# Three 256-column matmuls into one set of PSUM columns in place of a 512- and a 256-column matmul into two halves

## The chip, the cores and the metric

The kernel runs on one core of a Trainium2 chip. The metric is the device time of one execution in microseconds. Before the change it is 2729.07 us, the median of three runs (2727.39 to 2730.07).

## The reference

The reference is a forward pass of two different transformer-like blocks in float32 over 256 tokens of 2048 features, one after the other.

```python
# first block
h = rms_norm(x, norm_mix_g); proj = h @ w_in                 # 2048 x 14336
y_a = attention(q, k, v, rel_table) @ w_attn_o
y_b = rg_lru_branch(xr, gr, ...) @ w_lru_o
y_c = short_conv_branch(sc_b, sc_c, sc_x, ...) @ w_sc_o
x = x + (g_a * y_a + g_b * y_b + g_c * y_c) @ w_out          # gates: sigmoid(g_pre + gate_b)
x = x + square(relu(rms_norm(x, norm_mlp_g) @ w_mlp_up)) @ w_mlp_down
x = rms_norm(x, final_g)
# second block
h = rmsnorm(x, g_mix) @ w_in                                 # SSD, gate z, indexer, q, k, v
x = x + concat(y_ssd, y_att) @ w_out
x = x + square(relu(rmsnorm(x, g_mlp) @ w_up)) @ w_down      # 2048 x 8192 x 2048
```

Nearly all of the arithmetic is in the products of 256 tokens with weight matrices of 2048 rows or more.

## The kernel before

Activations are kept feature-major: a k-tile is 128 features by 256 tokens (T = 256). The products want more precision than one pass of TensorE gives in float32r, so both sides are split into a high and a low part. `Operand` holds the activations as [hi | lo], 512 columns per k-tile, and `stream` loads the weights (`raw`), makes `hi` on ScalarE (a cast) and `lo` on VectorE (a subtraction). Three products are added up: hi hi, hi lo and lo hi.

The work is a list of jobs. A job is a group of 512 output columns; its k-tiles come in chunks of two, 256 rows by 512 columns of the weight matrix, 512 KB in one transfer. `stream` walks over all chunks of all jobs; at each step it issues loads some steps ahead, splits the weights of a chunk ahead, calls `products` for the first pair of accumulators (`ps[0]`, 2 x 128 output features) and then for the second (`ps[1]`), and in between lets a stage of side work through (`side.tick`: norms, attention, recurrences) and a stage of the evacuations under way (`advance`). The evacuations are generators: each `yield` hands over until the next call of `advance`. The order of all instructions is the order in which they are emitted; a rough model of the engines' clocks (`Meter`) decides when side work is emitted.

A weight tile is 128 x 128 weights of one k-tile. Its weights are the stationary operand and the activations move past them. For each tile `products` issues two matmuls: `hi` of the weights against both halves of the activations, 512 columns, and `lo` of the weights against the high half, 256 columns, into the second half of the accumulator. An accumulator for 128 features is thus 512 columns of PSUM, a whole bank: the first half has hi hi, the second hi lo and lo hi. A pair of them takes two banks, and the pool `psm` has three such pairs; two more banks (`pss`) serve the side work.

When a group ends, `total` adds the halves: ScalarE copies the second half to `cr`, VectorE adds the first half to it and writes `tot`. What follows reads `tot`: a multiplication by the reciprocal norm (`keep`, `gate`), by a gate (`gated`), an addition to the residual (`residual`), a squared relu (`relu2`).

Jobs marked `tok` are token-major: the activations are stationary, the weights move, and all three products have 512 columns. These are the values of both attentions and the last quarter of the last product. In the trace all instructions of the engines have the line of one helper (L104), so that groups are told apart by their tiles: `ps<-h,hi` is a 512-column matmul of weights `hi` with operand `h`, and `ps<-h,lo` the 256-column one. `hm` is the operand of the products up, `hid` that of the products down; `mixop`, `ymix`, `ya`, `yb` and `yc` are those of the other products.

Of the kernel before, what the change touches and what calls it, by code (L numbers as in the profile page):

```python
# [10 lines left out]
F32 = mybir.dt.float32  # L11
# [14 lines left out]
# how far the vector and scalar engines may fall behind for side work, and shortly before a group of columns ends  # L26
MOST, LEAST = 9.0, 7.0
# what a stage of side work yields if the next one waits for nothing that the vector and scalar engines owe
FREE = "free"
# lanes of side work, the urgent ones first  # L30
LANES = ["norm", "small", "idx", "gate", "ssd", "k", "q", "att"]
# the second block's projections: SSD input, its gate z, indexer queries, queries, keys, values
# [3 lines left out]
class Operand:  # L36
    """Feature-major activations split exactly into two float32r parts: [hi | lo] per k-tile."""
# [20 lines left out]
class Job:  # L58
    """One group of output columns: chunks of two k-tiles stream past pairs of accumulators."""
# [9 lines left out]
class Meter:  # L69
    """An engine whose instructions are timed, roughly, as they are emitted: each starts when the engine is free and  # L70
    what it reads has been written."""
# [36 lines left out]
class Core:  # L108
# [8 lines left out]
    def behind(self):  # L117
        """How far the vector or scalar engine is behind the tensor engine."""
        return max(self.vector.clock, self.scalar.clock) - self.tensor.clock


class Side:
    """Work that runs between the steps of the main stream, in lanes: a lane's next stage is emitted once what its
    last one computes is ready, and while the vector and scalar engines aren't behind."""
# [20 lines left out]
    def bank(self, name):  # L145
        """The side banks take turns: the one that is next, free once its last tile has been read."""
        self.banks.append(name)
        old = self.banks.popleft()
        if old:
            self.core.free[name] = self.core.read.get(old, 0.0) + Meter.LATENCY  # L150
# [24 lines left out]
class Builder:  # L175
    def __init__(self, ctx, tc, d):
# [7 lines left out]
        self.psm = pool("psm", 3, space=PSUM)  # L184
# [21 lines left out]
    def vectors(self, name, st, specs):  # L206
        """Per-feature vectors, laid out as [feature in its tile, tile], by one transpose of their rows."""
# [12 lines left out]

    def wload(self, w, col):
        """Chunks of two k-tiles by 512 columns of w, from column col."""
        def load(raw, c):
            src = w[2 * P * c:2 * P * (c + 1), col:col + 512].rearrange("(k p) n -> p k n", p=P)
            self.nc.sync.dma_start(raw, src)
        return load

    def stream(self, jobs):
# [5 lines left out]
        for s, (j, c, i) in enumerate(steps):  # L234
# [26 lines left out]
            if first:  # L261
                ps = [self.psm.tile([P, 2, 512], F32, tag="main", name=f"ps{s}_{q}") for q in range(npair)]
                held = []
            op = j.op() if callable(j.op) else j.op
            # around a group's ends its first pair runs a step ahead, so that it starts and ends earlier
# [19 lines left out]
    def products(self, j, op, ps, q, c, hi, lo, first, last):  # L285
        """Two k-tiles past a pair of accumulators: hi hi, hi lo and lo hi."""
        nc = self.nc
        for m in range(2):
            o = ps[:, m, :]
            for kk in range(2):  # L290
# [9 lines left out]
                if a:  # L300
                    nc.tensor.matmul(o, hi[:, kk, w], op.both(k), start=True, stop=False)
                nc.tensor.matmul(o[:, T:], lo[:, kk, w], op.hi(k), start=False, stop=False)
                if not a:
                    nc.tensor.matmul(o, hi[:, kk, w], op.both(k), start=False, stop=z)

    def advance(self, newest=False, only=None):
        """One stage of the evacuations under way, or of the newest."""
# [10 lines left out]

    def total(self, ps, t=None):
        """The sum of both halves of a pair of accumulators."""  # L320
        nc = self.nc
        cr = self.tmp.tile([P, 2, T], F32, tag="cr", name="cr")
        nc.scalar.copy(cr, ps[:, :, T:])
        if t is None:
            t = self.tmp.tile([P, 2, T], F32, tag="tot", name="tot")
        nc.vector.tensor_tensor(t, ps[:, :, :T], cr, op=OP.add)
        return t
# [4 lines left out]
    def split(self, op, k, src):  # L332
        """k-tiles k and k + 1 of op from src [P, 2, T]."""
# [4 lines left out]
    def split_scaled(self, op, k, src, g):  # L338
        """k-tiles k and k + 1 of op from src times the per-feature g."""
# [13 lines left out]
    def squares(self, acc, k, src, g=None):  # L353
        """Adds the squares of a pair of tiles to acc [P, 2, T]."""
# [13 lines left out]
    def mean(self, acc, out=None, scale=1.0 / D):  # L368
        """Sums of the columns of acc times scale, token-major [P, 2]."""
# [9 lines left out]
    def rsqrt(self, out, v):  # L379
        """out = (v + EPS) ** -0.5, small: a guess from the exponent's bits, then Newton."""  # L380
# [13 lines left out]
    def row(self, out, col):  # L394
        """out [P, T] = col [P tokens, 2] laid along the free axis of every partition."""
# [16 lines left out]

    def load_x(self, load):
        """x, turned feature-major: h = x * norm_mix_g as an operand, x itself kept in DRAM."""
# [60 lines left out]
    def keep(self, dst, at, func=None, scaled=True):  # L475
        """Evacuates to tiles at + 2q of dst, times rstd, through func."""
        def evac(q, ps):
            k = at + 2 * q
            o = dst[k // 4][:, k % 4:k % 4 + 2, :]
            if not scaled:  # L480
                self.total(ps, o)
                return
            t = self.total(ps)
            yield
            self.side.drain("norm")
            self.nc.vector.tensor_tensor(t if func else o, t, self.pairwise(self.rstd), op=OP.mult)
# [4 lines left out]
    def keep_tok(self, dst, at):  # L491
        """Evacuates token-major to columns at of dst[token tile]."""
        def evac(q, ps):
            for t in range(2):
                self.nc.scalar.activation(dst[t][:, at:at + 512], ps[:, t, :], AF.Copy, scale=self.rstd_t[:, t:t + 1])
            yield
        return evac

    def gate(self, col, gt):
        """sigmoid(proj + gate_b)"""  # L500
        def evac(q, ps):
            nc = self.nc
            t = self.total(ps)
            g = gt()[:, 2 * q:2 * q + 2, :]
            yield
            nc.vector.tensor_tensor(t, t, self.pairwise(self.rstd), op=OP.mult)
# [5 lines left out]
    def gated(self, gt, mix, j, first, out=None):  # L512
        """mix += gate * y; with out, the sum is split into that operand."""
        def evac(q, ps):
            nc = self.nc
            t = self.total(ps)
            m = mix[j][:, 2 * q:2 * q + 2, :]
            g = gt()[:, 2 * q:2 * q + 2, :]
            yield
            if first:  # L520
                nc.vector.tensor_tensor(m, t, g, op=OP.mult)
            else:
                nc.vector.tensor_tensor(t, t, g, op=OP.mult)
# [6 lines left out]
    def t5_bias(self):  # L530
        """rel_table by distance, masked above the diagonal: [q, head, (128 keys of tile 0 | 256 of tile 1)]."""
# [12 lines left out]
        # 128 copies, 385 apart: read 384 apart, each query's row is the one before it moved by one key  # L544
# [12 lines left out]
    def softmax_rows(self, s):  # L557
        """Rows of s [P, 384]: queries of tile 0 over 128 keys, of tile 1 over 256; in place."""
# [16 lines left out]
    def probs(self, q, k, scale, bias, pt):  # L575
        """Transposed softmax of one head, into pt [P, 384]: scale(token tile), bias(token tile) [P, keys]."""
# [14 lines left out]
    def weigh(self, pt, v, out, k):  # L591
        """out tile k = v^T p^T, feature-major; v(token tile) is [tokens, 128 features]."""
# [19 lines left out]
    def causal_conv(self, out, src, w, bias, taps, col):  # L612
        """out [P, n, T] = causal depthwise convolution of src [P, n, T], two feature tiles at a time; w(tap) and bias
        per feature tile."""
# [18 lines left out]
    def lru_constants(self):  # L633
        """c4 = 4 softplus(-lambda): log a = -2 c4 r."""
# [14 lines left out]
    def log1p(self, out, e, z, z2):  # L649
        """log(1 + e) for 0 <= e <= 1, as 2 atanh(e / (2 + e))."""  # L650
# [21 lines left out]
    def lru(self, hf, xr, hs):  # L672
# [14 lines left out]
        # a = exp(-2 c4 r), and sqrt(1 - a^2) = (1 + a) sqrt(tanh(c4 r))  # L687
# [44 lines left out]
    def residual(self, j, scale=None, gvec=None, sq=(), op=None):  # L732
        """res += product (times scale); then squares and the next operand, res times gvec."""
        def evac(q, ps):
            nc = self.nc
            t = self.total(ps)
            yield
            k = 4 * j + 2 * q
            r = self.res[j][:, 2 * q:2 * q + 2, :]
            if scale is not None:  # L740
                nc.vector.tensor_tensor(t, t, self.pairwise(scale()), op=OP.mult)
            nc.vector.tensor_tensor(r, r, t, op=OP.add)
# [7 lines left out]
    def relu2(self, hidden, j):  # L750
        def evac(q, ps):
            nc = self.nc
            t = self.total(ps)
            nc.vector.scalar_tensor_tensor(t, t, 0.0, t, op0=OP.max, op1=OP.mult)
# [103 lines left out]
    def output(self, w, op, gvec, wait=None):  # L858
        """res += w^T op, then the operand of the feed-forward; with wait, each half of op for all columns in turn."""
# [38 lines left out]
    def feed_forward(self, up, down, last=None, after=None):  # L898
        """res += relu(hm up)^2 down times the squared reciprocal norm; last(j) prepares the next operand, or without
        it the last quarter is stored."""  # L900
# [25 lines left out]
    def first_end(self):  # L926
        """Evacuation of the first block: the last norm's and the next norm's statistics, the next operand."""
# [487 lines left out]
```

## Time and profile before

| what | value |
|---|---|
| time, median of 3 runs | 2729.07 us (2727.39 to 2730.07) |
| span of the profiled execution | 2727.0 us |
| TensorE (PE) busy | 2704.5 us, 99%, 15382 matmuls |
| weight loads (PEld) busy | 2345.9 us, 86%, 15382 loads |
| VectorE (DVE) busy | 1728.0 us, 63% |
| ScalarE (ACT) busy | 1281.9 us, 47% |
| mean granted TensorE clock | 0.999 |
| mean DMA traffic | 188 GB/s |

The span is the time from the first to the last instruction of one profiled execution, and the device time of a run has a little around it. Busy times are the union of an engine's instructions. Matmuls overlap in the pipeline, so the mean duration of one is longer than the distance from one start to the next; what a matmul costs is read from distances between starts, or from how many fit into a stretch without gaps. A group of instructions is followed by the idle time of its engine just before it and by what ended that idle time.

### The profile page before, as it was taken

Reading aid. Unit: us, or ns where it says so; the run is one execution under the profiler, and the core shown is the slowest. Engines: PE = TensorE matmul, PEld = TensorE weight load, DVE = VectorE, ACT = ScalarE, POOL = GpSimd, SP = SyncE. Lnnn points to the kernel's source line nnn. Section 1 sums busy time; section 2 is a strip of 40 time slices with the busy share of each in tenths; the row PEclk is TensorE's granted clock in tenths of the full one; section 3 lists DMA queues with packets and bytes.
Section 4 is the critical chain, followed back from the end, with each engine's and each line's share of the span. In section 5 each row is a group of like instructions: output and inputs, shape, how many; then the busy total and the mean of one; then the engine's idle time right before and its main releaser. Section 6 shows DMA issues by size and latency. Waiting matters only on the chain.

```text
span 2727.0 us, 38618 instructions
## 1 busy us (share of the span) xinstructions
PE 2704.5 (99%) x15382; PEld 2345.9 (86%) x15382; DVE 1728.0 (63%) x2331; ACT 1281.9 (47%) x1705; POOL 35.0 (1%) x70
## 2 busy tenths in 40 slices
PE   8999999999999999999999999999999999999999
PEld 7788888888888888888888888788888888888887
DVE  7565655656676655555566679687785555555554
ACT  5654544434555443444444455455564344344442
POOL 2000000000000000000000000000000000000000
PEclk9999999999999999999999999999999999999999
DMA  8755555655675656556565557455565555655644
GB/s 283 199 172 173 183 193 190 200 181 184 194 236 180 185 183 210 170 185 201 181 205 174 196 156 235 134 183 187 177 185 183 196 185 179 203 177 190 189 149 168
DMA packets 268660, 513.71 MB, mean 188 GB/s; under 512 B 22994, under 2 KB 23250, under 8 KB 268480
## 3 DMA queue, kind: packets, MB, share of 16 engines
q1 hardware_dynamic: 263360, 496.30, 56.8%
q0 software_dynamic: 4512, 12.84, 1.8%
q8 instruction: 121, 1.98, 0.3%
q10 hardware_dynamic: 608, 2.11, 0.2%
q14 instruction: 59, 0.48, 0.1%
HBM read 503.29 MB, written 7.88 MB: 187 GB/s over the span
## 4 chain that ended last, share of the span: by engine, by line
PE 96%; DMA 3%; issue 1%; DVE 1%; SPq 0%; ACT 0%; POOL 0%; DVEq 0%; POOLq 0%
PE ps L104 93%; DMA t5d<-by 1%; DMA raw<-w_in 1%; PE ix L104 0%; PE sc L104 0%; PE pv L104 0%; DMA bias<-t5d 0%; PE ps_row L104 0%; PE py L104 0%; PE pT L104 0%; PE hn L104 0%; DVE lo L104 0%; PE xT L104 0%; PE lg L104 0%; PE ps_mean L104 0%
## 5 line engine op out<-in xcount | busy, mean ns | idle before, releaser
L104 DVE TENSOR_TENSOR lo<-raw,hi 128x1024 fp32r<-128x1024 f32 (+1 forms) x944 | 1101.9, 1216 | 153.8 <-ACT hi L104 152.4
L104 ACT CAST hi<-raw 128x1024 fp32r<-128x1024 f32 (+1 forms) x944 | 926.6, 1044 | 80.4 <-DMA raw<-w_down 43.1
L104 PE MATMUL ps<-h,hi 128*128 128x512 f32 x2336 | 814.5, 396 | 7.4 <-DVE tot L104 5.6
L104 PE MATMUL ps<-hm,hi 128*128 128x512 f32 x2048 | 705.4, 394 | 0.0
L104 ACT COPY cr<-ps 128x512 f32<-128x512 f32 x241 | 141.3, 587 | 1093.9 <-PE ps L104 1093.9
L104 PE MATMUL ps<-h,lo 128*128 128x256 f32 x2336 | 635.3, 282 | 4.1 <-DVE lo L104 4.1
L104 DVE TENSOR_TENSOR tot<-ps,cr 128x512 f32<-128x512 f32 x230 | 158.4, 691 | 731.5 <-ACT cr L104 731.3
L104 PE MATMUL ps<-hid,hi 128*128 128x512 f32 x1792 | 615.0, 394 | 0.0
L104 PE MATMUL ps<-hm,lo 128*128 128x256 f32 x2048 | 548.5, 278 | 0.0
L104 PEld LDWEIGHTS ps<-h,hi 128*128 128x128 f32 x2336 | 430.9, 188 | 97.7 <-DVE tot L104 6.5
L104 PE MATMUL ps<-hid,lo 128*128 128x256 f32 x1792 | 478.3, 277 | 0.0
L104 PEld LDWEIGHTS ps<-h,lo 128*128 128x128 f32 x2336 | 441.2, 189 | 23.1 <-DVE lo L104 5.0
L104 PEld LDWEIGHTS ps<-hm,hi 128*128 128x128 f32 x2048 | 375.9, 188 | 78.2
L104 PEld LDWEIGHTS ps<-hm,lo 128*128 128x128 f32 x2048 | 384.8, 188 | 11.4
L104 PEld LDWEIGHTS ps<-hid,hi 128*128 128x128 f32 x1792 | 328.6, 188 | 68.3
L104 PEld LDWEIGHTS ps<-hid,lo 128*128 128x128 f32 x1792 | 336.4, 188 | 9.9
L104 PE MATMUL ps<-ymix,hi 128*128 128x512 f32 x256 | 89.3, 397 | 0.0
L104 PE MATMUL ps<-mixop,hi 128*128 128x512 f32 x256 | 87.9, 394 | 0.0
L104 PE MATMUL ps<-hi,hid 128*128 128x512 f32 x256 | 79.0, 389 | 0.0
L104 PE MATMUL ps<-mixop,lo 128*128 128x256 f32 x256 | 68.3, 277 | 0.0
L104 PE MATMUL ps<-ymix,lo 128*128 128x256 f32 x256 | 67.3, 283 | 0.0
L104 PE MATMUL ps<-hi,h 128*128 128x512 f32 x192 | 61.5, 395 | 0.0
(304 smaller groups left out, 1776.3 us busy)
## 6 DMA issues: line engine op xcount, KB each, us to landing
raw<-w_in SPq DMA_DIRECT2D x312, 512.0 KB, 4.1
raw<-w_mlp_up SPq DMA_DIRECT2D x128, 512.0 KB, 4.0
raw<-w_mlp_down SPq DMA_DIRECT2D x128, 512.0 KB, 4.6
raw<-w_up SPq DMA_DIRECT2D x128, 512.0 KB, 4.3
raw<-w_down SPq DMA_DIRECT2D x128, 512.0 KB, 4.5
raw<-w_out SPq DMA_DIRECT2D x64, 512.0 KB, 4.5
raw<-w_attn_o SPq DMA_DIRECT2D x16, 512.0 KB, 4.7
raw<-w_lru_o SPq DMA_DIRECT2D x16, 512.0 KB, 4.1
```

What stands on the lines that cost most here:

```text
L104: return f(out, *args, **kw)
```

## The change

In a tile of a job that is not token-major, `products` issues three matmuls of 256 columns, all into the same 256 columns of PSUM: `hi` of the weights with the high half, `lo` with the high half, `hi` with the low half. The two accumulators of a pair share a bank, so only the first matmul of the first of them has the start flag. `psm` has six tiles of one bank. `total` is gone: what followed it reads PSUM itself, mostly as the first operand of the VectorE instruction. In `relu2` ScalarE writes the relu of the sum to SBUF and VectorE multiplies the sum in PSUM by it, one step later. Token-major jobs get two tiles of one bank each; their matmuls stay as they are. The diff without its changes of comments, cut:

```diff
-        self.psm = pool("psm", 3, space=PSUM)
+        self.psm = pool("psm", 6, space=PSUM)
...
-                ps = [self.psm.tile([P, 2, 512], F32, tag="main", name=f"ps{s}_{q}") for q in range(npair)]
+                ps = [self.main_ps(f"ps{s}_{q}", j.tok) for q in range(npair)]
...
-            o = ps[:, m, :]
+            o = ps[m] if j.tok else ps[:, m, :]
...
-                if a:
-                    nc.tensor.matmul(o, hi[:, kk, w], op.both(k), start=True, stop=False)
-                nc.tensor.matmul(o[:, T:], lo[:, kk, w], op.hi(k), start=False, stop=False)
-                if not a:
-                    nc.tensor.matmul(o, hi[:, kk, w], op.both(k), start=False, stop=z)
+                nc.tensor.matmul(o, hi[:, kk, w], op.hi(k), start=a and m == 0, stop=False, skip_group_check=True)
+                nc.tensor.matmul(o, lo[:, kk, w], op.hi(k), start=False, stop=False, skip_group_check=True)
+                nc.tensor.matmul(o, hi[:, kk, w], op.lo(k), start=False, stop=z and m == 1, skip_group_check=True)
...
-    def total(self, ps, t=None):
-        nc = self.nc
-        cr = self.tmp.tile([P, 2, T], F32, tag="cr", name="cr")
-        nc.scalar.copy(cr, ps[:, :, T:])
-        if t is None:
-            t = self.tmp.tile([P, 2, T], F32, tag="tot", name="tot")
-        nc.vector.tensor_tensor(t, ps[:, :, :T], cr, op=OP.add)
-        return t
+    def main_ps(self, name, tok):
+        if tok:
+            return [self.psm.tile([P, 512], F32, tag="main", name=f"{name}_{t}") for t in range(2)]
+        return self.psm.tile([P, 2, T], F32, tag="main", name=name)
+    def tot(self):
+        return self.tmp.tile([P, 2, T], F32, tag="tot", name="tot")
...
             if not scaled:
-                self.total(ps, o)
+                self.nc.scalar.copy(o, ps)
                 return
-            t = self.total(ps)
-            yield
             self.side.drain("norm")
-            self.nc.vector.tensor_tensor(t if func else o, t, self.pairwise(self.rstd), op=OP.mult)
+            t = self.tot() if func else o
+            self.nc.vector.tensor_tensor(t, ps, self.pairwise(self.rstd), op=OP.mult)
+            yield
             if func:
                 self.nc.scalar.activation(o, t, func)
...
-            t = self.total(ps)
-            yield
             k = 4 * j + 2 * q
             r = self.res[j][:, 2 * q:2 * q + 2, :]
+            t = ps
             if scale is not None:
-                nc.vector.tensor_tensor(t, t, self.pairwise(scale()), op=OP.mult)
-            nc.vector.tensor_tensor(r, r, t, op=OP.add)
+                t = self.tot()
+                nc.vector.tensor_tensor(t, ps, self.pairwise(scale()), op=OP.mult)
+                yield
+            nc.vector.tensor_tensor(r, t, r, op=OP.add)
+            if scale is None:
+                yield
...
-            t = self.total(ps)
-            nc.vector.scalar_tensor_tensor(t, t, 0.0, t, op0=OP.max, op1=OP.mult)
+            t = self.tot()
+            nc.scalar.activation(t, ps, AF.Relu)
+            yield
+            nc.vector.tensor_tensor(t, ps, t, op=OP.mult)
             yield
             self.split(hidden, 4 * j + 2 * q, t)
```

`gate` and `gated` change in the same way as `keep`: the multiplication reads `ps`, and the `yield` comes after it.

## Rows read from the trace of the kernel before

**Rows 1.** The page, busy us (share of the span) x instructions of each engine.

```profile
PE 2704.5 (99%) x15382; PEld 2345.9 (86%) x15382; DVE 1728.0 (63%) x2331; ACT 1281.9 (47%) x1705; POOL 35.0 (1%) x70
```

**Rows 2.** Waits of PE: who waited for whom, us in total, times, longest.

```profile
PE ps L104 <- DVE tot L104: 5.6, 2, 5.1
```

**Rows 3.** View by windows: stretch, length, busy us (x instructions) by engine, PEclk, DMA.

```profile
600.00:900.00 300.00, 300.00 (x1732) 262.24 (x1731) 195.77 (x230) 147.89 (x199) 2.15 (x4) 1.00 0.61 197
```

**Rows 4.** Timeline of PE, operand hm: start us, duration us, instruction, count.

```profile
1499.71 0.39 PE L104 MATMUL ps<-hm,hi 128*128 128x512 f32 x1
1499.94 0.27 PE L104 MATMUL ps<-hm,lo 128*128 128x256 f32 x1
1500.05 0.40 PE L104 MATMUL ps<-hm,hi 128*128 128x512 f32 x1
...
1503.87 0.39 PE L104 MATMUL ps<-hm,hi 128*128 128x512 f32 x1
```

**Rows 5.** Groups of PE's instructions: busy us, mean ns, idle before and its releaser.

```profile
L104 PE MATMUL ps<-h,hi 128*128 128x512 f32 x2336 | 814.5, 396 | 7.4 <-DVE tot L104 5.6 <-ACT hi L104 1.8
L104 PE MATMUL ps<-hm,hi 128*128 128x512 f32 x2048 | 705.4, 394 | 0.0
...
L104 PE MATMUL ps<-hid,hi 128*128 128x512 f32 x1792 | 615.0, 394 | 0.0
...
L104 PE MATMUL ps<-mixop,hi 128*128 128x512 f32 x256 | 87.9, 394 | 0.0
...
L104 PE MATMUL ps<-ya,hi 128*128 128x512 f32 x128 | 44.2, 395 | 0.0
```

**Rows 6.** Timeline of PE, token-major end; the counts between are 2 and 1.

```profile
2650.19 0.62 PE L104 MATMUL ps<-hi,hid 128*128 128x512 f32 x2
2650.64 0.39 PE L104 MATMUL ps<-lo,hid 128*128 128x512 f32 x1
...
2654.95 0.62 PE L104 MATMUL ps<-hi,hid 128*128 128x512 f32 x2
```

**Rows 7.** Timeline of PE, first chunk of a group, two short matmuls in a row.

```profile
1494.26 0.40 PE L104 MATMUL ps<-hm,lo 128*128 128x256 f32 x2
1494.50 0.63 PE L104 MATMUL ps<-hm,hi 128*128 128x512 f32 x2
1494.96 0.39 PE L104 MATMUL ps<-hm,lo 128*128 128x256 f32 x2
1495.19 0.40 PE L104 MATMUL ps<-hm,hi 128*128 128x512 f32 x1
```

**Rows 8.** Timeline of the weight loads, PEld, operand hm.

```profile
1499.94 0.19 PEld L104 LDWEIGHTS ps<-hm,hi 128*128 128x128 f32 x1
1500.06 0.19 PEld L104 LDWEIGHTS ps<-hm,lo 128*128 128x128 f32 x1
```

**Rows 9.** Timeline of PE, eight matmuls of one column, and what follows.

```profile
1895.06 0.95 PE L104 MATMUL hn<-ones,sq 128*128 128x1 f32 x8
1895.87 0.90 PE L104 MATMUL sc<-k,q 128*128 128x128 f32 x4
```

**Rows 10.** Windows, then timeline of PE, while the clock was at half.

```profile
100.50:103.00 2.50, 2.50 (x8) 2.15 (x9) 2.50 (x4) 2.50 (x4) 0.00 (x0) 0.50 1.04 360
...
101.33 1.05 PE L104 MATMUL ps<-h,hi 128*128 128x512 f32 x2
102.18 0.63 PE L104 MATMUL ps<-h,lo 128*128 128x256 f32 x2
102.61 0.63 PE L104 MATMUL ps<-h,hi 128*128 128x512 f32 x1
```

**Rows 11.** Groups of the evacuation: busy us, mean ns, idle before and its releaser.

```profile
L104 ACT COPY cr<-ps 128x512 f32<-128x512 f32 x241 | 141.3, 587 | 1093.9 <-PE ps L104 1093.9
...
L104 DVE TENSOR_TENSOR tot<-ps,cr 128x512 f32<-128x512 f32 x230 | 158.4, 691 | 731.5 <-ACT cr L104 731.3
```

**Rows 12.** Timelines of ACT and of PE, end of the first group.

```profile
35.89 0.59 ACT L104 COPY cr<-ps 128x512 f32<-128x512 f32 x1 [0.16 <-PE ps L104]
...
39.90 0.60 PE L104 MATMUL ps_row<-ident,rstd_t 128*128 128x128 f32 x4
```

More of the change, by code (lines that the diff above doesn't have):

```diff
@@ L480, in evac @@
             if not scaled:
-                self.total(ps, o)
+                self.nc.scalar.copy(o, ps)
                 return
-            t = self.total(ps)
+            self.side.drain("norm")
+            t = self.tot() if func else o
+            self.nc.vector.tensor_tensor(t, ps, self.pairwise(self.rstd), op=OP.mult)
             yield
-            self.side.drain("norm")
-            self.nc.vector.tensor_tensor(t if func else o, t, self.pairwise(self.rstd), op=OP.mult)
             if func:
@@ L494, in evac @@
             for t in range(2):
-                self.nc.scalar.activation(dst[t][:, at:at + 512], ps[:, t, :], AF.Copy, scale=self.rstd_t[:, t:t + 1])
+                self.nc.scalar.activation(dst[t][:, at:at + 512], ps[t], AF.Copy, scale=self.rstd_t[:, t:t + 1])
             yield
@@ L502, in evac @@
             nc = self.nc
-            t = self.total(ps)
+            t = self.tot()
             g = gt()[:, 2 * q:2 * q + 2, :]
+            nc.vector.tensor_tensor(t, ps, self.pairwise(self.rstd), op=OP.mult)
             yield
-            nc.vector.tensor_tensor(t, t, self.pairwise(self.rstd), op=OP.mult)
             for i in range(2):
@@ L515, in evac @@
             nc = self.nc
-            t = self.total(ps)
             m = mix[j][:, 2 * q:2 * q + 2, :]
             g = gt()[:, 2 * q:2 * q + 2, :]
+            t = m if first else self.tot()
+            nc.vector.tensor_tensor(t, ps, g, op=OP.mult)
             yield
[L520 to L523, printed above, removed]
+            if not first:
                 nc.vector.tensor_tensor(m, m, t, op=OP.add)
@@ L735, in evac @@
             nc = self.nc
-            t = self.total(ps)
-            yield
             k = 4 * j + 2 * q
             r = self.res[j][:, 2 * q:2 * q + 2, :]
+            t = ps
             if scale is not None:
-                nc.vector.tensor_tensor(t, t, self.pairwise(scale()), op=OP.mult)
-            nc.vector.tensor_tensor(r, r, t, op=OP.add)
+                t = self.tot()
[4 more added lines that the diff above has]
+                yield
             if op is not None:
@@ L752, in evac @@
             nc = self.nc
-            t = self.total(ps)
-            nc.vector.scalar_tensor_tensor(t, t, 0.0, t, op0=OP.max, op1=OP.mult)
+            t = self.tot()
+            nc.scalar.activation(t, ps, AF.Relu)
+            yield
+            nc.vector.tensor_tensor(t, ps, t, op=OP.mult)
             yield
@@ L1251, in misc @@
             st["misc"] = self.slots.tile([P, 2, T], F32, tag="slot", name="misc")
-            self.total(ps, st["misc"])
+            self.nc.scalar.copy(st["misc"], ps)
             yield
@@ L1325, in evac @@
                 o = self.xt[j][:, t, :]
-                nc.vector.scalar_tensor_tensor(o, ps[:, t, :], self.rt[:, t:t + 1], o, op0=OP.mult, op1=OP.add)
+                nc.vector.scalar_tensor_tensor(o, ps[t], self.rt[:, t:t + 1], o, op0=OP.mult, op1=OP.add)
                 nc.sync.dma_start(y[:, t, 512 * j:512 * j + 512], o)
```

## The prediction, made before the change was built

> **What bounds the kernel now.** I read first the busy times of the engines. TensorE is busy for 2704.5 of 2727.0 us [rows 1], so 22.5 us of the span at most are waits of TensorE, and everything else in the kernel is hidden behind it as long as it stays hidden. The list of waits then says what is in those 22.5 us: of the work that the change touches, TensorE waited only for `tot`, twice, 5.6 us together, nearly all of it in one wait [rows 2]. So the question is what a weight tile costs on TensorE, and the evacuation matters only where it could become a wait.
>
> The view by windows gives the price of a tile. Between 600 and 900 us the granted clock is 1.00, which is the 2.4 GHz level, TensorE has no gap, and 1732 matmuls run [rows 3]: 300 / 1732 = 173.2 ns each, 346.4 ns for the two of a tile. The timeline agrees: from the long matmul at 1499.71 to the one at 1503.87 there are twelve tiles, 4.16 / 12 = 346.7 ns [rows 4]. I use 346.7. A tile has 512 + 256 = 768 columns, which is 320 ns at 2.4 GHz, so 26.7 ns of a tile are something other than columns.
>
> How often it is paid stands in the groups by line: 2336 + 2048 + 1792 tiles for `h`, `hm` and `hid`, 256 each for `mixop` and `ymix` (one row stands for both), 128 each for `ya`, `yb` and `yc` (one row for three) [rows 5]. That is 7072 tiles, 7072 x 0.3467 = 2452 us, 90% of the span. The token-major jobs are not touched.
>
> **The change, part by part.** *Columns.* The three products still have 3 x 256 = 768 columns. Nothing is saved or added here.
>
> *Instructions.* A tile goes from two matmuls and two weight loads to three of each: 7072 more matmuls and 7072 more loads, all on the engine that sets the end. What a matmul costs beside its columns is therefore the whole question, and the trace of before has no long run of 256-column matmuls that would show it. I bound it by three readings.
>
> First reading, from two steady streams. The token-major end is a stream of 512-column matmuls only: from 2650.19 to 2654.95 us there are 21, 4.76 / 21 = 226.7 ns each [rows 6]. The mixed stream has one of 512 and one of 256 in 346.7 ns. If a 512-column matmul costs the same in both, the 256-column one costs 346.7 - 226.7 = 120.0 ns. The difference between the two sizes is then 106.7 ns for 256 columns, which is exactly one column a cycle at 2.4 GHz, and both sizes carry the same 13.3 ns on top. That the two streams fall on one such line is what I find strongest. A tile of three would cost 3 x 120.0 = 360.0 ns, 13.3 more than now.
>
> Second reading, from the recorded starts. In the mixed stream the short matmul starts at 1499.94 and the next long one at 1500.05 [rows 4]: 0.11 us, not 0.12, and the long one takes the rest. At a group's first chunk two short ones follow each other: 1494.26 to 1494.50 and 1494.96 to 1495.19, so 0.24 and 0.23 us for two, 117 ns each [rows 7]. By this, three cost 352 ns, 5 more than now; by the 0.11 us alone, 330 to 340. Against this reading: a start is recorded when one matmul gives way to the next, and if that moment lies some ns later after a long matmul than after a short one, the starts split the pair unevenly while its sum stays right.
>
> Third reading, the load. Every matmul loads 128 x 128 weights anew. Loads are recorded with 0.19 us, but they start 0.12 us apart (1499.94, 1500.06) [rows 8], so the record is longer than what a load occupies. Eight matmuls of a single column, each with a load of its own, take 1895.06 to 1895.87 us [rows 9], 0.10 us each, so a load can follow a load at about that pitch, which is just under the 107 ns of 256 columns. The load hides, but with nothing to spare. At the 1.2 GHz level the picture differs: with the clock at 0.50, two short matmuls take 102.18 to 102.61, 0.43 us, and two long ones 0.85 us, which is the columns alone [rows 10]. The 13.3 ns are thus a cost that shows only at the full clock, when a load and 256 columns are nearly equally long; the changed kernel will be at that point in every matmul. This too makes me take 120 ns.
>
> The Trainium skill speaks to the load as well: Perfetto Trace Analysis, section Identifying the Most-Contended Engine, says to judge TensorE by the busy share of LDWEIGHTS, since the busy time of matmuls misleads. That share is 86% here, and 7072 more loads at their recorded 0.188 us would make it 3676 us, more than the present span. The trace disagrees with taking it so, since loads overlap [rows 8].
>
> So: 7072 x (360.0 - 346.7) = 7072 x 13.3 ns = +94 us. Bounds: at 113 ns a matmul 7072 x (339 - 346.7) = -54 us; at 117 ns +30 to +40 us; at 120 ns +94 us.
>
> *Evacuation.* The 241 copies `cr` (141.3 us of ScalarE) go, except that 64 come back as a Relu in `relu2` and 11 as plain copies; the 230 additions `tot` (158.4 us of VectorE) go with them [rows 11]. The multiplications that followed read PSUM in place of `tot`. Both engines wait, not TensorE: 1093.9 us before `cr`, 731.5 us before `tot` [rows 11]. I cost this at nothing; the cover is TensorE's stream, and without it it would be worth part of those 300 us. `relu2` reads its PSUM tile one step later than before, but a pair of accumulators now takes one bank, so six pairs are in flight where there were three. That should end the 5.1 us wait [rows 2], at 100 us, a gain of up to 5.6 us.
>
> *A wait that is added.* `keep` now drains the norm before its first read, at the end of the first group, where it used to add the halves first and drain a step later. In the trace the first pair's copy runs at 35.89 us and the matmuls `ps_row` that need the norm at 39.90 us [rows 12]. The matmuls of the second pair, queued behind `ps_row` on TensorE, would wait for the norm up to 4.0 us; waiting for them are only their own evacuations. The kernel then stands in line for transfers until 100 us anyway. I set the gain of 5.6 against the 4.0 and count zero, keeping -6 and +4 for the range.
>
> *DMA.* No transfer is added or moved; a slower TensorE asks for weights more slowly.
>
> The sum by the profiled execution is 2727.0 + 94 = 2821 us of span. The median of the three runs, 2729.07, lies 2.1 us above that span, so 2823 us.
>
> **The rivals.** (a) The short matmul really costs what its starts show, 117.5 ns: 352.5 ns a tile, 7072 x 5.8 = +41 us, 2770 us. For it: [rows 7]. Against it: it makes the long matmul 232 ns here and 226.7 in the other stream.
>
> (b) On the other side, faster: a 256-column matmul costs 115 ns or less when it stands among its like, as the 0.11 us steps say [rows 4], and the long matmul is the dear one. Then 345 ns a tile, -12 us, 2717 us; at 113 ns -54 us, 2675 us. It decides below 115.6 ns a matmul, a third of 346.7. For it: a load pitch of 0.10 us leaves room. Against it: the exact line through the two streams.
>
> (c) Loads don't overlap when all matmuls are short, and each tile costs 3 x 188 = 564 ns: 7072 x 217 = +1535 us, about 4264 us. The Trainium skill's rule on the LDWEIGHTS share points this way. Against it: loads 0.12 us apart [rows 8].
>
> (d) The new evacuations hold TensorE up (the norm's drain, or `relu2` with its later read) by more than 10 us on top of 120 ns a matmul: over 2835 us. Against it: over 700 us of waiting on either engine [rows 11] and twice the pairs in flight.
>
> **How the numbers follow.** The 120 ns case has 0.60, (a) 0.13, (b) 0.20, (c) 0.02, (d) 0.05. A change of 0.2%, 5.5 us, is about what can be told here. Slower: 0.60 + 0.13 + 0.02 + 0.05, and since a part of (a) touches no change and (b) begins there, 0.76 slower, 0.04 the same, 0.20 faster. The range must reach into (b), so 2700 to 2838: it holds (a), the upper half of (b) and the likeliest case with its bounds of -6 and +4 widened to 15 on top, and leaves out the lower half of (b), (c) and most of (d), 0.17. The likeliest case alone is 2815 to 2832.
>
> **What would show it.** Right: a window without gaps holds about 300 / 0.120 = 2500 matmuls in 300 us, against 1732 [rows 3], at granted clock 1.00; the matmul count is 22454; TensorE stays at 99%; `cr` is gone, and VectorE and ScalarE fall while the span grows. Wrong: starts of 0.113 to 0.115 us in a row of short matmuls, over 2600 in such a window; or gaps on TensorE released by the new evacuations; or loads further apart than the matmuls need. My number falls if the cost beside the columns belongs to the long matmul and not to each.

## The result, and the profile after

The changed kernel takes 2812.82 us, the median of four runs (2811.01 to 2813.01), against 2728.67 us before (four runs, 2727.39 to 2730.07): a ratio of 1.0307, 95% interval 1.0292 to 1.0321, 84 us slower. The forecast was 2823 us, slower. So sign and size hold; the likeliest case by itself, 2815 to 2832, is missed by 2 us at its lower end, and some 10 us of the forecast loss are not there (9 us, if a tile of before is put at the 346.9 ns of the steady stages and not at 346.7).

The page of the changed kernel, busy times as in [rows 1], shows who pays:

```profile
PE 2791.5 (99%) x22454; PEld 2748.1 (98%) x22454; DVE 1563.0 (56%) x2090; ACT 1214.3 (43%) x1539; POOL 35.7 (1%) x70
```

TensorE's busy time grows by 87.0 us and its idle time falls from 22.5 to 19.5 us. VectorE gives back 165 us and ScalarE 68 us, and nothing comes of it. The window of [rows 3], and one at the token-major end (length, busy us and instructions by engine, granted clock, DMA):

```profile
600.00:900.00 300.00, 300.00 (x2502) 300.00 (x2501) 167.78 (x189) 124.34 (x156) 2.15 (x4) 1.00 0.58 188
2730.00:2790.00 60.00, 60.00 (x266) 49.69 (x266) 28.94 (x27) 18.87 (x19) 0.00 (x0) 1.00 0.51 174
```

2502 matmuls in 300 us without a gap are 119.9 ns each. The token-major ones of 512 columns have kept their price: the window has 60 / 266 = 225.6 ns, with those that its ends cut counted whole, and by starts 15 of them go by from 2735.02 to 2738.42 us, 226.7 ns each. In the timeline of TensorE (start, duration, instruction, count) three tiles, nine matmuls, go by from 1489.38 to 1490.46:

```profile
1489.38 0.40 PE L104 MATMUL ps<-hm,hi 128*128 128x256 f32 x2
1489.62 0.28 PE L104 MATMUL ps<-hm,lo 128*128 128x256 f32 x1
1489.74 0.40 PE L104 MATMUL ps<-hm,hi 128*128 128x256 f32 x2
1489.98 0.28 PE L104 MATMUL ps<-hm,lo 128*128 128x256 f32 x1
...
1490.46 0.40 PE L104 MATMUL ps<-hm,hi 128*128 128x256 f32 x2
```

1.08 / 3 = 0.360 us a tile, where [rows 4] has 0.3467. The groups of the new evacuation, as in [rows 11], wait for TensorE as those of before did:

```profile
L104 DVE TENSOR_TENSOR tot<-ps,rrow 128x512 f32<-128x512 f32 x56 | 38.7, 692 | 291.4 <-PE ps L104 291.4
L104 ACT ACTIVATE tot<-ps 128x512 f32<-128x512 f32 x64 | 38.2, 597 | 411.1 <-PE ps L104 411.1
```

TensorE's list of waits no longer has `tot` [rows 2]. Two waits for a norm have come in its place:

```profile
PE ps_row L104 <- DVE rstd_t L104: 3.5, 1, 3.5
PE ps_row L104 <- DVE s_t L104: 3.3, 1, 3.3
```

The timeline shows the first of them at the place where [rows 12] has `ps_row`, and the window right behind it shows what it drags along:

```profile
36.13 0.28 PE L104 MATMUL ps<-h,hi 128*128 128x256 f32 x1
39.88 1.19 PE L104 MATMUL ps_row<-ident,rstd_t 128*128 128x128 f32 x4 [3.47 <-DVE rstd_t L104]
```

```profile
38.50:46.00 7.50, 6.12 (x30) 6.15 (x31) 2.14 (x9) 4.56 (x5) 1.84 (x2) 0.54 0.71 208
```

The granted clock is 0.54 over these 7.5 us. In the last 1.1 us of the wait it falls to the 1.2 GHz level, and TensorE then works at that level for 5.7 us, until 45.6 us. At the wait for `s_t`, which ends at 1681.04, the same happens from 1680.6 to 1684.0 us, 2.9 us of it with work.

### The profile page after: what moved, and what is told of

It is laid out like the page before. It is cut to its first block, busy times and chain, and to the rows that moved or that the text cites. A ratio compares the mean times of both kernels' runs of the same rounds, so it can differ in the third digit from the quotient of the medians.

```text
span 2811.0 us, 52565 instructions
## 1 busy us (share of the span) xinstructions
PE 2791.5 (99%) x22454; PEld 2748.1 (98%) x22454; DVE 1563.0 (56%) x2090; ACT 1214.3 (43%) x1539; POOL 35.7 (1%) x70
## 4 chain that ended last, share of the span: by engine, by line
PE 99%; DVE 1%; DMA 0%; issue 0%; ACT 0%; DVEq 0%; ACTq 0%
PE ps L104 96%; PE ix L104 0%; PE sc L104 0%; PE pv L104 0%; PE xT L104 0%; PE lg L104 0%; PE ps_row L104 0%; PE py L104 0%; PE pT L104 0%; DMA xt<-x 0%; PE hn L104 0%; DVE lo L104 0%; DVE ra L104 0%; PE ps_mean L104 0%; PE xst L104 0%
## 5 line engine op out<-in xcount | busy, mean ns | idle before, releaser
L104 PE MATMUL ps<-h,hi 128*128 128x256 f32 x4672 | 865.1, 285 | 1.8 <-ACT hi L104 1.8
L104 PEld LDWEIGHTS ps<-h,hi 128*128 128x128 f32 x4672 | 737.7, 193 | 7.8 <-issue 4.1
L104 PE MATMUL ps<-hm,hi 128*128 128x256 f32 x4096 | 741.4, 283 | 0.0
L104 PE MATMUL ps<-hid,hi 128*128 128x256 f32 x3584 | 646.3, 283 | 0.0
L104 PEld LDWEIGHTS ps<-hm,hi 128*128 128x128 f32 x4096 | 640.3, 192 | 0.0
L104 PEld LDWEIGHTS ps<-hid,hi 128*128 128x128 f32 x3584 | 559.6, 192 | 0.0
L104 PE MATMUL ps<-ymix,hi 128*128 128x256 f32 x512 | 95.0, 285 | 0.0
L104 PE MATMUL ps<-mixop,hi 128*128 128x256 f32 x512 | 92.3, 283 | 0.0
L104 PEld LDWEIGHTS ps<-ymix,hi 128*128 128x128 f32 x512 | 80.6, 192 | 0.1
L104 PEld LDWEIGHTS ps<-mixop,hi 128*128 128x128 f32 x512 | 79.9, 192 | 0.0
```

What stands on the lines that cost most here:

```text
L104: return f(out, *args, **kw)
```

## The experiments

Two theories of the price went into the runs. Theory 1 is the prediction's: every matmul carries 13.3 ns beside its columns, whatever its size, and the load of its weights is hidden. Theory 2: what is paid beside the columns grows with them (6.7 ns for each 256), and 256 columns are dear because a matmul can't be shorter than the load that it needs; the load is then the bound of the changed kernel. Both give 120.0 ns for 256 columns and 226.7 for 512, so other sizes and other loads have to tell them apart. A second question was where the missing 9 us are.

### The three products alone

The kernel before, with its halves, its `total` and its two-bank pairs, but three matmuls of 256 columns:

```diff
-                nc.tensor.matmul(o, hi[:, kk, w], op.both(k), ...)
-                nc.tensor.matmul(o[:, T:], lo[:, kk, w], op.hi(k), ...)
+                nc.tensor.matmul(o[:, :T], hi[:, kk, w], op.hi(k), ...)
+                nc.tensor.matmul(o[:, T:], lo[:, kk, w], op.hi(k), ...)
+                nc.tensor.matmul(o[:, T:], hi[:, kk, w], op.lo(k), ...)
```

> The three 256-column matmuls alone: hi hi goes to the first half of the accumulator, lo hi and hi lo to the second, and the two-bank pairs, the copy and the addition stay as they were. Theory 1 (each matmul costs its columns plus 13.3 ns): 360.0 ns a tile where the steady stages of the kernel before show 346.9, 7072 x 13.1 = +93 us, 2821 to 2823 us, and the wait for tot of about 5 us near 100 us is still there; the missing 9 us of the changed kernel's gain over this sum come from its evacuations and its smaller pairs. Rival (the price is one of writing three times into one set of columns, not of the count): well under 360 ns a tile, below 2790 us.

It takes 2813.12 us (four runs, 2812.90 to 2813.63), ratio 1.0308 [1.0292, 1.0323]: the same as the whole change. The expected 2821 to 2823 fell, and with it the idea that the new evacuation had saved the missing 9 us. The rival fell too: here the products go to two sets of columns, and the price of a matmul is the same. The window and the list of waits:

```profile
600.00:900.00 300.00, 300.00 (x2502) 300.00 (x2501) 187.32 (x216) 139.63 (x183) 2.14 (x4) 1.00 0.60 188
```

```profile
PE ps L104 <- DVE tot L104: 4.8, 1, 4.8
```

The loss lies in the matmuls alone, the same 2502 in 300 us. The `tot` wait of before is still here, with the clock at half for 6.8 us around 100 us. In the changed kernel the two norm waits stand in its place, so that the new evacuation changes nothing in sum.

### Two matmuls of 384 columns

```diff
-                nc.tensor.matmul(o[:, T:], lo[:, kk, w], op.hi(k), ...)
-                if not a: nc.tensor.matmul(o, hi[:, kk, w], op.both(k), ...)
+                nc.tensor.matmul(o[:, :384], lo[:, kk, w], op.both(k)[:, :384], ...)
+                if not a: nc.tensor.matmul(o[:, :384], hi[:, kk, w], op.both(k)[:, :384], ...)
```

> Two matmuls a tile, both of 384 columns (768 in all, as before): the second half of the low activations meets no high weights and the first half meets the low weights too, so that part of the computation is changed. Theory 1 (columns at 2.4 GHz plus 13.3 ns each): 2 x 173.3 = 346.7 ns a tile, the time of before, 2725 to 2732 us. Theory 2 (a column of float32r takes 17/16 of a cycle, and 256-column matmuls are held at 120 ns by their weight loads): 2 x 170.0 = 340.0 ns, 7072 x 6.7 = 47 us less, about 2681 us.

2753.72 us (two runs), ratio 1.009 [1.007, 1.011]. A stretch of the timeline with 32 matmuls of 384 columns between its ends:

```profile
1414.80 0.33 PE L104 MATMUL ps<-hid,hi 128*128 128x384 f32 x1
1414.97 0.33 PE L104 MATMUL ps<-hid,lo 128*128 128x384 f32 x1
...
1420.34 0.56 PE L104 MATMUL ps<-hid,hi 128*128 128x384 f32 x2
```

5.54 / 32 = 173.1 ns, as theory 1 has it (160 + 13.3) and not the 170.0 of theory 2. The total is some 24 us over its expectation because the first k-tile of each group keeps its 512-column matmul, 53 ns more, which I had left out: the trace has 482 of them, 482 x 53 ns = 26 us.

### One of 512 and two of 128 columns

```diff
-                nc.tensor.matmul(o[:, T:], lo[:, kk, w], op.hi(k), ...)
+                for h in range(2):
+                    nc.tensor.matmul(o[:, T + h * P:T + (h + 1) * P], lo[:, kk, w], op.hi(k)[:, h * P:(h + 1) * P], ...)
```

> The kernel before with its 256-column matmul cut into two of 128: three matmuls a tile of 512, 128 and 128 columns. Theory 1: 226.7 + 2 x 66.7 = 360.0 ns a tile, the same as the changed kernel's tile, about 2822 us. Theory 2 (a load is worth 112 to 120 ns, and a matmul shorter than that waits for the next load): 226.7 + 2 x (112 to 120) = 451 to 467 ns, 7072 x (104 to 120) = +740 to +850 us, 3470 to 3580 us. A time beyond that would mean that matmuls of 128 columns stream more slowly than one column a cycle.

3484.39 us (one run), as theory 2 said; theory 1's 2822 is off by 660 us. Window and timeline:

```profile
600.00:900.00 300.00, 300.00 (x1974) 270.58 (x1974) 137.37 (x153) 100.56 (x127) 0.00 (x0) 1.00 0.46 141
```

```profile
1399.64 0.45 PE L104 MATMUL ps<-hm,hi 128*128 128x512 f32 x1
1399.93 0.33 PE L104 MATMUL ps<-hm,lo 128*128 128x128 f32 x2
1400.10 0.45 PE L104 MATMUL ps<-hm,hi 128*128 128x512 f32 x1
```

1974 matmuls are 658 tiles of 456 ns. If the long one stays at 226.7, two matmuls of 128 columns take 229, so 114 to 115 ns each, where their columns are 53 ns. That points to a floor under a matmul with a fresh load. The starts would give 0.29 us to the long matmul and 0.17 to the two short ones, 85 ns each, which the next run contradicts.

### Four of 192 columns

In all k-tiles but a group's first:

```diff
+                for i, (u, x) in enumerate(((hi, op.hi(k)), (lo, op.hi(k)), (hi, op.lo(k)), (lo, op.lo(k)))):
+                    nc.tensor.matmul(o[:, :192], u[:, kk, w], x[:, :192], ...)
```

> The changed kernel with four matmuls of 192 columns in place of three of 256, 768 columns as before, in all k-tiles but the first of a chunk order (15 of 16 for most jobs); which columns meet which is changed, so the sums differ. Theory 1 alone (columns plus 13.3 ns): 4 x 93.3 = 373.3 ns a tile, +13.3 on 15/16 of 7072 tiles, about 2900 us. Theory 1 with a floor of about 113.5 ns under each matmul, which the run with 128 columns points to (two short ones in 229.5 ns): 4 x 113.5 = 454 ns a tile, +94 ns on 15/16 of 7072 tiles = +623 us, about 3435 us. If 128 columns are dear for another reason than a floor, 373.3 ns stand.

3375.45 us (one run), against 2900 by 13.3 ns on top of the columns and 3435 by the floor. The timeline from 1401.75 to 1402.97, eleven matmuls, has 1.22 / 11 = 111 ns each:

```profile
1401.75 0.27 PE L104 MATMUL ps<-hm,lo 128*128 128x192 f32 x1
...
1402.97 0.28 PE L104 MATMUL ps<-hm,hi 128*128 128x192 f32 x1
```

The floor is there, at 111 to 115 ns. It is under the 120.0 of 256 columns, so it isn't the whole of their price. That it is the load which sets it was not tried with narrower loads at these sizes.

### The same weights twice in a row

The changed kernel with the order hi hi, hi lo, lo hi, so that one load of three brings the weights that are there already:

```diff
-                nc.tensor.matmul(o, lo[:, kk, w], op.hi(k), ...)
-                nc.tensor.matmul(o, hi[:, kk, w], op.lo(k), ...)
+                nc.tensor.matmul(o, hi[:, kk, w], op.lo(k), ...)
+                nc.tensor.matmul(o, lo[:, kk, w], op.hi(k), ...)
```

> The changed kernel with its three matmuls in the order hi hi, hi lo, lo hi, so that two in a row have the same weights. Theory (each matmul loads its weights whatever was loaded before): 120.0 ns each, 360.0 ns a tile, 2811 to 2815 us, no change against the changed kernel. Rival (a load of the weights that are in the array already costs less): up to 13.3 ns less a tile, down to about 2720 us.

2812.73 us (four runs, 2812.20 to 2813.34), ratio 1.0305 [1.0288, 1.0323], and again 2502 matmuls from 600 to 900 us. Loading the same weights again costs as much as loading others.

### Smaller loads

In four kernels the moving columns of each matmul are left as they are and the loaded weights are made narrower. A matmul then also writes only as many rows of PSUM as it has columns of weights, and no run here separates the two; "the load" below stands for both. The changed kernel, and in the same way the kernel before and the one with 384 columns (these two also keep a group's last k-tile whole), with 64 columns of weights:

```diff
+                if not a:
+                    w = slice((2 * q + m) * P, (2 * q + m) * P + 64)
+                    o = ps[:64, m, :]
```

> The changed kernel with weights of 64 columns instead of 128 in all k-tiles but the first, so that half of the output features are left out of the sums there. The moving side keeps 256 columns and three matmuls a tile. Theory 1 (the 13.3 ns belong to the matmul): 120.0 ns each, 2810 to 2815 us. Rival (the 13.3 ns are a load that 256 columns don't hide): with half the load 107 to 110 ns each, 3 x (10 to 13) ns on 15/16 of 7072 tiles, 200 to 260 us less, 2550 to 2615 us.

2689.1 us (one run). Five tiles of the timeline:

```profile
1399.75 0.39 PE L104 MATMUL ps<-hid,hi 128*64 128x256 f32 x2
1399.97 0.28 PE L104 MATMUL ps<-hid,lo 128*64 128x256 f32 x1
...
1401.45 0.39 PE L104 MATMUL ps<-hid,hi 128*64 128x256 f32 x2
```

1.70 / 15 = 113.3 ns: neither the 120.0 of theory 1 nor the 107 to 110 of its rival. So 6.7 of the 13.3 ns go with the narrower load, and 6.7 stay. The kernel before with such loads:

> The kernel before (512 and 256 columns a tile) with weights of 64 columns instead of 128 in all k-tiles but the first and the last of a group, so that half of the output features are left out of the sums there. Theory 3 (a load takes its time from the moving stream in proportion to the columns that it loads, 13.3 ns for 128 and 6.7 for 64, however long the matmul beside it is): 226.7 - 6.7 + 120.0 - 6.7 = 333.3 ns a tile where it was 346.7, on 14/16 of 7072 tiles -83 us, about 2646 us. Rival (the 6.7 ns of the run with 256-column matmuls came from a load that 256 columns just fail to hide; beside 512 columns the size of the load is without effect): only the 256-column one gains, -41 us, about 2688 us, or nothing, 2729 us.

2687.45 us (two runs), ratio 0.9849 [0.982, 0.9878]. In the timeline five tiles take 1.70 us, 340.0 ns each:

```profile
1399.73 0.39 PE L104 MATMUL ps<-hid,hi 128*64 128x512 f32 x1
1399.96 0.27 PE L104 MATMUL ps<-hid,lo 128*64 128x256 f32 x1
...
1401.43 0.39 PE L104 MATMUL ps<-hid,hi 128*64 128x512 f32 x1
```

That is 6.7 ns less than in [rows 4], not twice as much. With the 113.3 of the run above for the short one, 226.7 are left for the long one, which then doesn't gain. With the price of a tile now equal in both, two matmuls and three give the same time, 2687 and 2689 us.

> The run with two matmuls of 384 columns a tile, with weights of 64 columns instead of 128 in all k-tiles but the first and the last of a group, so that half of the output features are left out of the sums there. Theory 4 (a column of float32r takes 17/16 of a cycle, 6.7 ns more for 256 columns, 10 for 384, 13.3 for 512, and what is above that is a load of 128 that the matmul does not quite hide, 6.7 ns beside 256 columns, 3.3 beside 384, none beside 512): 170.0 ns each, 6.7 ns a tile less on 14/16 of 7072 tiles, -41 us against 2753.7, about 2712 us. Rival (the cost goes in steps, 6.7 ns for each 256 columns begun, and a load of 128 is hidden beside 384 columns): 173.3 ns each as before, about 2754 us.

2756.29 us (one run), no gain over the 2753.72 of the full loads. From 1404.32 to 1421.33 there are 98 matmuls, 17.01 / 98 = 173.6 ns (four of them with full loads):

```profile
1404.32 0.34 PE L104 MATMUL ps<-hid,hi 128*64 128x384 f32 x1
...
1421.33 0.34 PE L104 MATMUL ps<-hid,hi 128*64 128x384 f32 x1
```

Beside 384 columns, as beside 512, the load is hidden. The changed kernel with loads of 32 columns:

> The changed kernel with weights of 32 columns instead of 128 in all k-tiles but the first of a group, so that three quarters of the output features are left out of the sums there. Theory 3: 106.7 + 3.3 = 110.0 ns a matmul, 330 ns a tile on 15/16 of 7072 tiles, -199 us against the changed kernel, about 2614 us. Rival (a matmul of 256 columns has a floor of about 112 to 113 ns whatever is loaded): 113.3 ns as with 64 columns, about 2689 us.

2731.01 us (one run), slower than with 64, which no theory had:

```profile
600.00:900.00 300.00, 300.00 (x2549) 276.84 (x2548) 170.79 (x192) 127.26 (x159) 2.15 (x4) 1.00 0.62 194
1200.00:1500.00 300.00, 300.00 (x2636) 285.88 (x2635) 156.13 (x163) 123.95 (x136) 0.00 (x0) 1.00 0.61 193
```

In the second stretch it has the 113.8 ns of the loads of 64 (a group's first k-tile, with full loads, is in the mean), in the first 117.7. The trace has two steady prices of a tile and little between: 340.0 ns as with loads of 64, and 353.3 ns (24 tiles from 702.51 to 710.99 us). So a still smaller load saves nothing more, and a steady stream of equal matmuls can run at either of two prices; what decides between them is open.

### The norm a step later

The changed kernel with one more `yield` ahead of the drain in `keep`, so that the second pair's matmuls are emitted before `ps_row`, as they were before the change:

```diff
+            yield
             self.side.drain("norm")
             t = self.tot() if func else o
```

> The changed kernel with one more yield ahead of the drain of the norm in keep, so that the matmuls ps_row are emitted a step later, as in the kernel before. Theory: the two waits of TensorE for the norm (3.5 and 3.3 us) go, and with them the stretches at half clock that follow each (6.8 and 3.4 us long, half of which is lost): 3.5 + 3.4 + 3.3 + 1.7 = up to 12 us less than the changed kernel, 2801 to 2808 us. Rival: the stall only moves to the next transfer, which is late anyway in the first 100 us: 2809 to 2813 us.

2801.93 us (four runs, 2801.19 to 2802.36), ratio 1.0265 [1.0248, 1.0282], 10.9 us under the changed kernel. The window that was at half clock, and the list of waits from its head:

```profile
38.50:46.00 7.50, 7.32 (x61) 7.12 (x60) 7.22 (x15) 5.12 (x6) 0.00 (x0) 1.00 1.04 342
```

```profile
PE ps_x L104 <- DMA vst<-norm_mix_g: 3.9, 1, 3.9
PE ps L104 <- DVE lo L104: 3.0, 6, 1.0
```

61 matmuls run where there were 30. Both norm waits are gone and the clock is whole. The 2801.93 us lie within the 2801 to 2808 expected. It is the fastest of the kernels with three matmuls of 256 columns that leave nothing out, and still 72 us slower than before. I found none that beats the kernel before.

## Why the prediction was right, step by step

**The price of a tile (first reading).** Right in its number: 360.0 ns a tile, 120.0 a matmul. What it was made of was not quite as I put it ("both sizes carry the same 13.3 ns on top"). The runs give, in ns for a matmul at granted clock 1.00:

| columns | columns alone | loads of 128 | loads of 64 |
|---|---|---|---|
| 128 | 53.3 | 114 to 115 | |
| 192 | 80.0 | 111 | |
| 256 | 106.7 | 120.0 | 113.3 |
| 384 | 160.0 | 173.1 | 173.6 |
| 512 | 213.3 | 226.7 | 226.7, if the short one has 113.3 |

The rows of 256 columns or more fit one account: 6.7 ns for each 256 columns begun, so twice for 384 and 512, and 6.7 ns more where a load of 128 stands beside only 256. It was written down ahead of the run with 384 columns and loads of 64, and held there. It is a fit to three sizes and not a mechanism: where between 256 and 384 the step lies was not measured, and the dearer stretches with loads of 32 don't follow it. A tile of before is then 320 + 3 x 6.7 + 6.7 = 346.7 ns with one matmul that doesn't hide its load, a tile of after 320 + 3 x 6.7 + 3 x 6.7 = 360.0 with three. The 13.3 ns of difference are two loads that show. Under theory 1 it would have been one more matmul's 13.3: the same number, and two steady streams can't tell them apart. The number held because the subtraction 346.7 - 226.7 gives the price of a short matmul whatever it is made of. That the two sizes lay on one exact line, which I found strongest, was luck: by this account one carries 6.7 + 6.7 and the other 2 x 6.7. Theory 1 fell as a rule for all sizes with the 128 columns, and as the account of 256 with the loads of 64; theory 2 fell with the 384 columns.

**The starts (second reading).** Rightly set aside, and rivals (a) and (b) with it. The runs with 128 and 192 columns show that the starts split a tile's time wrongly: 85 ns by the starts for a matmul of 128 columns, where a stream of 192 alone runs at 111.

**The load (third reading).** "The load hides, but with nothing to spare" is the step that failed in its first half: beside 256 columns the load of 128 shows with 6.7 ns. The trace of before already spoke against it, and I misread it. The 0.10 us between loads is a mean over eight steps [rows 9], and the first step is short: the second matmul starts at 1895.09, 26 ns after the first, whose load had stood beside a matmul of 512 columns. The last six of the eight, taken alone, and what follows them:

```profile
1895.20 0.81 PE L104 MATMUL hn<-ones,sq 128*128 128x1 f32 x6
1895.87 0.36 PE L104 MATMUL sc<-k,q 128*128 128x128 f32 x1
```

That is 0.67 / 6 = 112 ns a step, over the 107 ns of 256 columns and not under it, and it agrees with the 111 to 115 ns of 128 and 192 columns. For rival (b), too, the load left less room than I wrote.

The Trainium skill speaks of the overlap in TensorE: Matmul & The Clock Gate, section Step-by-step: what each phase is for: loading the next weights takes no SBUF read bandwidth from the running matmul, since the two have read ports of their own. Beside 384 and 512 columns the runs show no cost of the load; beside 256 they do, 120.0 against 113.3 ns, and by what path no run shows. The section LDWEIGHTS (loading the stationary operand) of that page of the Trainium skill gives P / 1.2 for P columns, an estimate of 107 ns for 128; the floor measured here is 111 to 115 ns.

**Loads that don't overlap (rival c).** The recorded busy share of loads rises from 86% to 98% and no tile takes 564 ns. The recorded durations overlap; a share near 100% here stands for a loss of 3%. The 3676 us of the prediction add a sum of durations to a busy time in which overlaps are merged. Summed alike, the loads of before come to 15382 x 0.188 = 2892 us, already more than the span.

**The evacuation at nothing.** Right. The cover held: the engines that evacuate waited for TensorE by hundreds of us, and their 233 us of work less show nowhere: the run with the three products alone keeps that work and takes the same time. The `tot` wait went, as expected.

**A wait that is added.** The wait of the second pair's matmuls was put at up to 4.0 us and measured 3.5. What I missed is the second block's norm, another 3.3 us through the same `keep`, and the half clock at both. TensorE works at that level for 5.7 + 2.9 = 8.6 us. There five tiles take 3.20 us (41.94 to 45.14), 640 ns each and not 360, so some 3.8 us are lost. Before, it was 2.9 us of work behind the `tot` wait [rows 10], 1.3 us lost. My zero for all of this came out as -3.0 of idle time and +2.5 of clock: near zero, but by luck, since the terms are not mine. The run with the norm a step later shows the price of the added waits: 10.9 us, close to 3.5 + 3.3 + 3.8. Rival (d) had the place right, but no sum over 2835 came of it.

**The missing 9 us.** By the same instruction 256 tiles apart in the steady stages, a tile goes from 346.9 to 360.0 ns, so 7072 tiles give +93; idle time and clock give -0.5. Some 100 interruptions of the stream by side work (three `pT` transposes, for example, go from 347 to 320 ns from the starts around them) give about -3. Of the difference to +84 some 5 to 6 us remain. Most of it lies in a reading of mine: not every tile of before cost 346.9 ns. In the stages with side work, stretches of its trace without any gap are dearer, as in these 48 tiles:

```profile
2593.86 0.40 PE L104 MATMUL ps<-hm,hi 128*128 128x512 f32 x1
...
2610.82 0.40 PE L104 MATMUL ps<-hm,hi 128*128 128x512 f32 x1
```

16.96 / 48 = 353.3 ns a tile. Some 710 tiles of before run at this price, 711 x 6.4 ns = 4.6 us that the kernel had paid already; in the changed kernel, and in the one with the three products alone, tiles have 360.0 ns in these stages as elsewhere. About 1 us is left unexplained, and what puts the stream of before at the dearer price isn't shown.

## What to carry to other kernels

Where TensorE sets the end, count matmuls and loads before anything else: 7072 more of each, with not one column more, cost 84 us, and 233 us of work taken from VectorE and ScalarE returned nothing, because TensorE never waited for it. Price a matmul by how many fit into a stretch without gaps, and by streams of different sizes, not by recorded durations or single starts; and if two streams give a number, vary the load and the columns separately before believing what the number is made of. A mean over a few merged instructions can hide one step that is unlike the others: take the first one off before reading a pitch from it. When an evacuation is shortened by a step, look at what its first read drains: work emitted one step earlier put 3.5 and 3.3 us of waiting on TensorE, and the lower clock at them cost about 4 us more.

## What was not expected of the hardware

At the full clock a matmul with a fresh load of 128 x 128 took 111 to 115 ns in the streams of 128 and 192 columns (53 and 80 ns of columns), and 112 ns with a single column. From 256 columns on the cost beside the columns fits 6.7 ns for each 256 begun, not one fixed amount for each matmul, and a load of 128 columns shows with 6.7 ns beside 256 columns and with nothing beside 384. At the 1.2 GHz level neither is seen: 640 ns a tile are its 768 columns. A steady stream without gaps can also run at more than one price: tiles of before at 346.9 or 353.3 ns, tiles with loads of 32 at 340.0 or 353.3. Why the steps are what they are, why the load's 6.7 ns come on top of a floor that lies lower than 120, and what chooses between two prices, stays open. Whether a 512-column matmul can write its two halves into the same 256 columns of PSUM, which would save the adding without a third matmul, wasn't tried.
